# Causal mask as a matrix product, and q and k turned by DMA, in a fused decoder layer

## The chip, the cores and the metric

One core of one Trainium2 chip runs the whole layer. The metric is device time in microseconds (us) of one launch. A core has a tensor engine (PE), a vector engine (DVE), a scalar engine (ACT), GpSimd (POOL) and a sync engine (SP) that only issues transfers. Each engine works through its own instructions in the order in which they stand; ACT, SP and POOL also issue transfers (DMAs), each from its own queue. What an engine waits for at the head of its queue holds up everything behind it.

## What is computed

The layer has 1024 positions of width 1024. What matters here is its attention part: 8 heads of 64, in float32, with normalised q and k, a forget term added to the scores, a causal mask and a softmax.

```python
h = rms_norm(x, attn_norm_g)
q, k, v, f_logit, cb, cc, cu, ga, gb = jnp.split(h @ w_in, offs, axis=-1)
q = rms_norm(q.reshape(b, s, 8, 64), q_norm_g)
k = rms_norm(k.reshape(b, s, 8, 64), k_norm_g)
c = jnp.cumsum(log_sigmoid(f_logit + b_f), axis=1)
logits = einsum('bhqd,bhkd->bhqk', q, k) * 64 ** -0.5
logits = logits + (c[..., :, None] - c[..., None, :])
logits = where(key_pos <= q_pos, logits, -1e30)
y_att = einsum('bhqk,bhkd->bhqd', softmax(logits), v)
y_conv = cb * causal_short_conv(cc * cu, conv_w)
x = x + (sigmoid(ga) * (y_att @ w_out_att) + sigmoid(gb) * (y_conv @ w_out_conv)) @ w_o
```

A mixture of 16 experts and a gated embedding follow; the change does not touch them.

## The kernel before

Every float32 product is made of fp16 products: a value is split into a high and a low fp16 part (`split`, L113: ACT rounds, DVE takes the rest). The stage in question fills the first 480 us of the run.

**Blocks.** `project` (L224) makes q, k and v for one pair of heads and 128 tokens: 24 products of 384 columns into one PSUM bank named acc (two such banks). ACT squares q and k (L235), DVE sums (L237) and scales (L110), POOL takes the power -0.5 (L111), DVE writes the normalised `qn` (L240), then ACT and DVE write V (L243, L244). V at L244 is the last reader, and frees the bank. There are 32 blocks, 8 for each of 4 pairs; the first 8 run ahead of the loop over units.

**Turning q and k.** For every second block, `finish` (L249) has PE turn the two `qn` tiles, which are float32, with four transposes of 128x128 into a bank named tr. Six ACT and six DVE instructions then write Qh, Ql and K with a head's dimensions along partitions, the gains folded in (L259 to L265).

**Units.** `attend_s` (L298) makes the scores of one head and 256 queries; there are 32 units. SP loads a row of forget terms from memory to all partitions: `base` (three buffers) and again `own` (one buffer) for the half of the queries whose last 128 keys end earlier. POOL adds the causal mask to `own` (L306), DVE to `base` (L307). PE makes two products for each piece of up to 512 keys (L319, L320) into one of three banks named s; DVE adds base or own and takes the row maximum in the same instruction (L321); ACT takes the exponential (L330). Each half then has its own reciprocal (L331, L332), a split into `hl` (L335, L336) and a DMA transpose on SP into `pTr` (L338). `attend_v` (L341) multiplies pTr by V two units later.

**Filler.** `filler` (L444) interleaves products of 512 columns for the convolution and gates, L122 to L124, in runs of 24 that use the same two acc banks. Their weights (`fraw`, two buffers, L404) and the weights of the next pair (`wraw`, three buffers, L207) are loaded on SP too.

**Order.** In this stage the program is handed to a scheduler that interleaves the generators' work and fixes one order for each engine before the run. The loop that feeds it stands at L507 to L527:

```python
for n in range(len(units)):
    fills.append(scores(n + 2))
    proj = block_in(n + LEAD)
    fills.append(block_out(n + LEAD - 1))
    fills.append(itertools.islice(extra, 8 * fill_halves(n)))
    weave(values(n), units[n][1] + 1, itertools.chain(*fills), total)
```

So a block is projected eight turns of the loop ahead (LEAD = 8), and scores are made two units ahead.

Of the kernel before, what the change touches and what calls it, by code (L numbers as in the profile page):

```python
# [19 lines left out]
S = 1024  # L20
D = 1024
# [22 lines left out]
OWN = 1  # L44
# [5 lines left out]
QS = 16.0  # L50
KS = 4.0
# [5 lines left out]
NEG = -1e30  # L57


QNB = 3  # L60
# [3 lines left out]
def trunk_layer(ctx: ExitStack, tc: tile.TileContext, x, wq0, wq, wc, wgb, wga, wA, wB, wo, wr,  # L64
# [25 lines left out]
    gq = const.tile([128, 1], F32, name="gq")  # L90
    nc.vector.tensor_scalar(gq, vt[:, 0:1], DH ** -0.5 * QS, None, op0=ALU.mult)
    gk = const.tile([128, 1], F32, name="gk")
    nc.vector.tensor_scalar(gk, vt[:, 1:2], KS, None, op0=ALU.mult)
# [83 lines left out]
    mask = ap_.tile([128, 128], F32, name="mask")  # L177
    nc.gpsimd.memset(mask, 0.0)
    nc.gpsimd.affine_select(mask, mask, pattern=[[-1, 128]], compare_op=ALU.is_ge, fill=NEG,
                            base=0, channel_multiplier=1)  # L180

    def tokens_load(t):
        xt = ap_.tile([128, D], F32, name="P", bufs=5)
        nc.sync.dma_start(xt, x[t * 128:(t + 1) * 128, :])
        return xt
# [12 lines left out]
    def wq_raw(p, k):  # L198
        if p == 0 and k > 2:
            raw = (ap_.tile([128, S], F32, name="hl", bufs=3) if k < 6 else  # L200
                   ap_.tile([128, 2 * S], F32, name="pTr", bufs=3))[:, :392]
# [22 lines left out]
    def project(p, t, w, ws, V, fz):  # L224
# [13 lines left out]
        rsqrt(ss[:, 4:8], ss[:, 0:4], DH, [128, 4], EPS * PS * PS)  # L238
# [8 lines left out]
        st8["qn", p * NT + t] = qn  # L247

    def finish(s, qns, Qh, Ql, K):  # L249
        tok = slice(s * 256, (s + 1) * 256)  # L250
        tr = tr_bank()
        t4 = tr.rearrange("p (n t) -> p n t", n=2)
        for i, qn in enumerate(qns):
            for n in range(2):
                nc.tensor.transpose(t4[:, n, i * 128:(i + 1) * 128],
                                    qn[:, 2 * n:2 * n + 2].rearrange("p h d -> p (h d)"), identF)
        for hd in range(2):
            a, b = [slice(64 * i, 64 * i + 64) for i in (hd, 1 - hd)]
            nc.scalar.activation(Qh[a, hd], t4[a, 0], AF.Copy, scale=gq[a])  # L259
            nc.vector.scalar_tensor_tensor(Ql[a, hd], t4[a, 0], gq[a], Qh[a, hd], op0=ALU.mult, op1=ALU.subtract)  # L260
            nc.scalar.activation(K[a, hd, tok], t4[a, 1], AF.Copy, scale=gk[a])
            nc.vector.scalar_tensor_tensor(K[b, hd, tok], t4[a, 1], gk[a], K[a, hd, tok],
                                           op0=ALU.mult, op1=ALU.subtract)
            nc.scalar.activation(Qh[b, hd], Qh[a, hd], AF.Copy)
            nc.vector.tensor_copy(Ql[b, hd], Ql[a, hd])  # L265

    def forget(hf, fz):
# [18 lines left out]
        rows = [ap_.tile([128, S], F32, name="P", bufs=5) for _ in range(2)]  # L286
# [11 lines left out]
    def attend_s(p, s, hd, Qh, Ql, K):  # L298
# [3 lines left out]
        last = chunks(s, 0)[-1][0]  # L302
        w = 256 * s + 128 - last
        own = ap_.tile([128, 384], F32, name="own", bufs=OWN)
# [3 lines left out]
        pT_ = ap_.tile([128, 8, 2, 256], FP16, name="pTr", bufs=3)  # L308
        for i in range(2):
            qt = 2 * s + i  # L310
            nk = (qt + 1) * 128
            pt = ap_.tile([128, S], F32, name="P", bufs=5)
            st = ap_.tile([128, 8], F32, name="st", bufs=4)
            q = slice(i * 128, (i + 1) * 128)
            nch = 0
            for c0, cw in chunks(s, i):
                valid = min(cw, nk - c0)
                sb = s_bank()
                nc.tensor.matmul(sb[:, :cw], lhsT=Qh[:, hd, q], rhs=K[:, hd, c0:c0 + cw], start=True, stop=False)  # L319
                nc.tensor.matmul(sb[:, :cw], lhsT=Ql[:, hd, q], rhs=K[:, hd, c0:c0 + cw], start=False, stop=True)  # L320
                nc.vector.tensor_tensor_reduce(  # L321
                    out=pt[:, c0:c0 + valid], in0=sb[:, :valid], in1=own[:, :valid] if i == 0 and c0 == last else base[:, c0:c0 + valid], scale=1.0,
                    scalar=-3e38, op0=ALU.add, op1=ALU.max, accum_out=st[:, nch:nch + 1])
                nch += 1
                yield cw
            if nch == 2:
                nc.vector.tensor_scalar(st[:, 2:3], st[:, 0:1], st[:, 1:2], -1.0 / (QS * KS), op0=ALU.max, op1=ALU.mult)  # L327
            else:
                nc.vector.tensor_scalar(st[:, 2:3], st[:, 0:1], -1.0 / (QS * KS), None, op0=ALU.mult)
            nc.scalar.activation(pt[:, :nk], pt[:, :nk], AF.Exp, bias=st[:, 2:3], scale=1.0 / (QS * KS), accum_out=st[:, 3:4])  # L330
            nc.vector.tensor_scalar(st[:, 4:5], st[:, 3:4], 1.0 / GS, None, op0=ALU.mult)  # L331
            nc.vector.reciprocal(st[:, 5:6], st[:, 4:5])  # L332
            hl = ap_.tile([128, 8, 2, 128], FP16, name="hl", bufs=3)
            p3 = pt[:, :nk].rearrange("p (k m) -> p k m", m=128)
            nc.scalar.activation(hl[:, :qt + 1, 0], p3, AF.Copy, scale=st[:, 5:6])  # L335
            nc.vector.scalar_tensor_tensor(hl[:, :qt + 1, 1], p3, st[:, 5:6], hl[:, :qt + 1, 0], op0=ALU.mult,  # L336
                                           op1=ALU.subtract)
            nc.sync.dma_start_transpose(pT_[:, :qt + 1, :, q], hl[:, :qt + 1].rearrange("p k a m -> p (k a m)"))  # L338
        st8["P", p * 8 + 2 * s + hd] = pT_

    def attend_v(p, s, hd, P, V):  # L341
# [9 lines left out]
        yl = ap_.tile([128, 256], F32, name="yl", bufs=1)  # L351
# [10 lines left out]
    def block_in(m):  # L362
        p, t = blocks[m]
        if t == 0:
            W8[p] = load_wq(p, raw0 if p == 0 else None)
            st8["K", p] = ap_.tile([128, 2, S], FP16, name="K", bufs=2)
            st8["V", p] = ap_.tile([128, 2, 8, 128], FP16, name="V", bufs=2)
        if t % 2 == 0:
            s = t // 2
            st8["Q", p, s] = (ap_.tile([128, 2, 256], FP16, name="Qh", bufs=4),  # L370
                              ap_.tile([128, 2, 256], FP16, name="Ql", bufs=4))
            if p == 0 and s % 2 == 0:
                st8["f", s // 2] = ap_.tile([128, 4, 8], F32, name="fz", bufs=2)
        yield from project(p, t, *W8[p], st8["V", p], st8.get(("f", t // 4)))

    def block_out(m):
        p, t = blocks[m]
        if t % 2:
            finish(t // 2, [st8.pop(("qn", i)) for i in (m - 1, m)], *st8["Q", p, t // 2], st8["K", p])
# [3 lines left out]
        if t % 2:  # L383
            yield 430

    def scores(n):
        p, s, hd = units[n]
        yield from attend_s(p, s, hd, *st8["Q", p, s], st8["K", p])
# [82 lines left out]
    for i in range(WARM):  # L471
        nc.tensor.matmul(warm[:, :128], lhsT=identB, rhs=identB, start=True, stop=True)
    for t in range(2):
# [35 lines left out]
    for n in range(len(units)):  # L509
# [843 lines left out]
def layouts(i):  # L1353
# [49 lines left out]
    o["gains"] = np.stack([a["attn_norm_g"][0], a["ffn_norm_g"][0]])  # L1403
# [24 lines left out]
```

## Time and profile before

| | |
|---|---|
| median of 3 runs | 1128.04 us (1127.67 to 1128.4) |
| time of the profiled execution | 1129.68 us |
| its span in the trace | 1128.0 us |
| PE busy | 1051.3 us (93%) |
| DVE busy | 709.2 us (63%) |
| ACT busy | 563.5 us (50%) |
| POOL busy | 189.4 us (17%) |

The span is what the trace covers; 1.7 us lie around it. A matmul's busy time is modelled and overlaps with the next one's, so the cost of one matmul in a row of them is read from the distance of two starts. The granted clock of PE is given as a share: 1.00 is 2.4 GHz and 0.50 is 1.2 GHz. In the timeline the brackets hold the time that the engine stood idle before the instruction, and what ended it. The line numbers are those of the kernel before.

### The profile page before, as it was taken

The page shows a single profiled execution, that of the slowest core. Times are in us where ns is not written, and L with a number is a line of the kernel's source. Part 1 is how long each engine was busy: PE and PEld are TensorE (multiplying, and loading weights), DVE is VectorE, ACT ScalarE, POOL GpSimd, SP SyncE. Part 2 cuts the span into 40 slices and gives each one's busy share as a digit, 9 for nine tenths or more (in the row PEclk, how much of TensorE's full clock was granted, in tenths as well). Part 3 has the DMA queues.
Part 4 walks back from the last instruction along what each step waited for, and adds up shares of the span by engine and source line. Part 5 has one row for each costly group of instructions (what it writes and reads, how often), then busy time and mean ns, then how long its engine had stood idle before and what let it go on. Part 6 is the DMA issues. An engine that isn't in the chain of part 4 may idle for free. (4 is left out here: it accounts for less than half of the span.)

```text
span 1128.0 us, 18292 instructions
## 1 busy us (share of the span) xinstructions
PE 1051.3 (93%) x6776; PEld 607.1 (54%) x6776; DVE 709.2 (63%) x1603; ACT 563.5 (50%) x1033; POOL 189.4 (17%) x247
## 2 busy tenths in 40 slices
PE   7878998998999999999998999987989999998798
PEld 5544454554455544444443355546766777764354
DVE  7777765677766764032307745874978888855633
ACT  7665455565554653222215433445766777753232
POOL 3311011111211000000003422242201111005300
PEclk9979898999999999999999999988989999999999
DMA  8055456565665583152348650149999899727511
GB/s 310 24 129 143 105 124 157 126 129 138 152 129 117 138 179 93 53 176 87 112 154 259 207 211 38 57 135 371 388 383 302 306 334 325 236 78 235 180 53 56
DMA packets 135135, 195.46 MB, mean 173 GB/s; under 512 B 83010, under 2 KB 94794, under 8 KB 134914
## 3 DMA queue, kind: packets, MB, share of 16 engines
q1 hardware_dynamic: 118290, 141.40, 42.9%
q0 software_dynamic: 7632, 27.07, 7.3%
q10 hardware_dynamic: 9120, 25.78, 5.9%
q8 instruction: 54, 0.88, 0.3%
q14 instruction: 39, 0.32, 0.1%
HBM read 142.75 MB, written 32.59 MB: 155 GB/s over the span
## 5 line engine op out<-in xcount | busy, mean ns | idle before, releaser
L122 PE MATMUL acc<-hTh,fwh 128*128 128x512 f16 x336 | 127.3, 379 | 0.1
L124 PE MATMUL acc<-hTh,fwl 128*128 128x512 f16 x336 | 127.3, 379 | 0.0
L123 PE MATMUL acc<-hTl,fwh 128*128 128x512 f16 x336 | 127.3, 379 | 0.0
L961 DVE SCALAR_TENSOR_TENSOR wl<-wraw,wh 128x1024 f16<-128x1024 f32 x64 | 77.5, 1219 | 23.9 <-ACT wh L956 23.2
L230 PE MATMUL acc<-wqh,hTh 128*128 128x384 f16 (+1 forms) x248 | 83.0, 335 | 7.0 <-DVE V L244 4.7
L116 DVE SCALAR_TENSOR_TENSOR wl<-wraw,wh 128x1024 f16<-128x1024 f32 x47 | 57.4, 1232 | 51.0 <-ACT wh L115 49.5
L231 PE MATMUL acc<-wqh,hTl 128*128 128x384 f16 (+1 forms) x248 | 83.0, 335 | 0.8 <-DVE hTl L116 0.8
L232 PE MATMUL acc<-wql,hTh 128*128 128x384 f16 (+1 forms) x248 | 83.0, 334 | 0.2 <-DVE wql L116 0.2
L956 ACT ACTIVATE wh<-wraw 128x1024 f16<-128x1024 f32 x64 | 66.9, 1052 | 19.5 <-PE acc L1041 10.6
L330 ACT ACTIVATE P<-P,st 128x128 f32<-128x128 f32 (+3 forms) x64 | 49.2, 769 | 50.5 <-DVE st L327 38.2
L115 ACT ACTIVATE wh<-wraw 128x1024 f16<-128x1024 f32 x47 | 49.1, 1054 | 50.2 <-PE acc L123 26.4
L335 ACT ACTIVATE hl<-P,st 128x128 f16<-128x128 f32 (+3 forms) x64 | 48.8, 770 | 38.4 <-issue 15.8
L336 DVE SCALAR_TENSOR_TENSOR hl<-P,st,hl 128x128 f16<-128x128 f32 (+3 forms) x64 | 52.0, 818 | 12.6 <-ACT hl L335 12.2
L1324 PE MATMUL acc<-wh,xl 128*128 128x512 f16 (+1 forms) x136 | 50.4, 371 | 5.7 <-DVE xl L116 5.7
L1041 PEld LDWEIGHTS <-wh 128*128 128x128 f16 x512 | 51.5, 101 | 4.2 <-issue 0.8
L124 PEld LDWEIGHTS <-fwl 128*128 128x128 f16 x336 | 32.9, 98 | 38.3
L1040 PEld LDWEIGHTS <-wh 128*128 128x128 f16 x512 | 52.1, 102 | 1.9 <-issue 0.3
L111 POOL TENSOR_TENSOR ss<-ss,mh 128x4 f32<-128x4 f32 x32 | 37.6, 1176 | 91.5 <-DVE ss L110 87.3
L122 PEld LDWEIGHTS <-fwh 128*128 128x128 f16 x336 | 32.9, 98 | 34.8
L123 PEld LDWEIGHTS <-fwh 128*128 128x128 f16 x336 | 32.9, 98 | 34.5 <-issue 0.3
L1325 PE MATMUL acc<-wl,xh 128*128 128x512 f16 (+1 forms) x136 | 50.4, 370 | 0.0
L1323 PE MATMUL acc<-wh,xh 128*128 128x512 f16 (+1 forms) x136 | 50.4, 370 | 0.0
(319 smaller groups left out, 2621.8 us busy)
## 6 DMA issues: line engine op xcount, KB each, us to landing
wraw<-in_we_dram SPq DMA_DIRECT2D x96, 512.0 KB
Yd<-yt ACTq DMA_DIRECT2D x14, 512.0 KB
fraw<-in_wc_dram SPq DMA_DIRECT2D x12, 512.0 KB
wraw<-in_wq_dram SPq DMA_DIRECT2D x24, 192.0 KB
P<-in_x_dram SPq DMA_DIRECT2D x8, 512.0 KB
fraw<-in_wga_dram SPq DMA_DIRECT2D x8, 512.0 KB
base<-brow SPq DMA_DIRECT2D x8, 512.0 KB
sga<-fg POOLq DMA_DIRECT2D x8, 512.0 KB, 5.9
```

Of the source, the lines that this page charges most:

```text
L116: nc.vector.scalar_tensor_tensor(lo, src, scale, hi, op0=ALU.mult, op1=ALU.subtract)
L122: nc.tensor.matmul(acc, lhsT=whi, rhs=xhi, start=k == 0, stop=False)
L123: nc.tensor.matmul(acc, lhsT=whi, rhs=xlo, start=False, stop=False)
L124: nc.tensor.matmul(acc, lhsT=wlo, rhs=xhi, start=False, stop=k == nk - 1)
L230: nc.tensor.matmul(acc[:, :w], lhsT=hTh[:, k, tok], rhs=wh[:, :w], start=k == 0, stop=False)
L231: nc.tensor.matmul(acc[:, :w], lhsT=hTl[:, k, tok], rhs=wh[:, :w], start=False, stop=False)
L232: nc.tensor.matmul(acc[:, :w], lhsT=hTh[:, k, tok], rhs=wl[:, :w], start=False, stop=k == 7)
L336: nc.vector.scalar_tensor_tensor(hl[:, :qt + 1, 1], p3, st[:, 5:6], hl[:, :qt + 1, 0], op0=ALU.mult, op1=ALU.subtract)
L956: nc.scalar.activation(wh, raw, AF.Copy, scale=HS)
L961: V_.scalar_tensor_tensor(wl, raw, HS, wh, op0=ALU.mult, op1=ALU.subtract)
L1040: nc.tensor.matmul(a[:, :n], lhsT=wh[:, k], rhs=xT[:, k, 0, :n], start=k == 0, stop=False)
L1041: nc.tensor.matmul(a[:, :n], lhsT=wh[:, k], rhs=xT[:, k, 1, :n], start=False, stop=False)
```

## The change

Four edits go together.

1. **q and k in rows.** The transposes and splits of `finish` are gone. `project` now scales and splits q and k while tokens lie along partitions: POOL multiplies `qn` by a gain tile, ACT and DVE write `rows`, fp16 of 128 x 768 (six groups of 128 columns; k's gain is folded into q's), and one DMA transpose on SP for each block writes them into `KQ`. The scaling at L110 moves from DVE to POOL for these blocks.
2. **Mask as a product.** A matrix of -60000 above the diagonal is multiplied by 60000 times the identity and added to the scores in PSUM by one product of 128 columns for each half unit. `own` is gone, with its load, and so are both mask additions.
3. **Queues.** The loads of `base`, of the filler's weights and of the next pairs' weights are issued on POOL instead of SP.
4. **Smaller ones.** The reciprocals of a unit's two halves are one instruction of two columns; `P` has 4 buffers for 5, `hl` 2 for 3, `qn` 2 for 3; scale factors QS and KS change places.

```diff
-    def finish(s, qns, Qh, Ql, K):
...
-                nc.tensor.transpose(t4[:, n, i * 128:(i + 1) * 128],
-                                    qn[:, 2 * n:2 * n + 2].rearrange("p h d -> p (h d)"), identF)
...
-            nc.scalar.activation(Qh[a, hd], t4[a, 0], AF.Copy, scale=gq[a])
-            nc.vector.scalar_tensor_tensor(Ql[a, hd], t4[a, 0], gq[a], Qh[a, hd], op0=ALU.mult, op1=ALU.subtract)
...
-        rsqrt(ss[:, 4:8], ss[:, 0:4], DH, [128, 4], EPS * PS * PS)
+        rsqrt(ss[:, 4:8], ss[:, 0:4], DH, [128, 4], EPS * PS * PS, nc.gpsimd)
...
+        nc.gpsimd.tensor_tensor(qn, qn, gqk, op=ALU.mult)
+        rows = ap_.tile([128, 2, 3, 2, DH], FP16, name="rows", bufs=2)
+        nc.scalar.activation(rows[:, :, 0, 0], qn[:, 2:4], AF.Copy)
+        nc.vector.tensor_tensor(rows[:, :, 0, 1], qn[:, 2:4], rows[:, :, 0, 0], op=ALU.subtract)
+        q2 = qn[:, 0:2, None, :].to_broadcast([128, 2, 2, DH])
+        nc.scalar.activation(rows[:, :, 1], q2, AF.Copy)
+        nc.vector.tensor_tensor(rows[:, :, 2], q2, rows[:, :, 1], op=ALU.subtract)
+        nc.sync.dma_start_transpose(KQ[:, :, tok], rows.rearrange("p h j a d -> p (h j a d)"))
...
-        nc.sync.dma_start(base[:, :n], brow[s][2 * p + hd:2 * p + hd + 1, :].to_broadcast([128, n]))
...
-        nc.sync.dma_start(own[:, :w], brow[s][2 * p + hd:2 * p + hd + 1, last:last + w].to_broadcast([128, w]))
-        nc.gpsimd.tensor_tensor(own[:, w - 128:w], own[:, w - 128:w], mask, op=ALU.add)
-        nc.vector.tensor_tensor(base[:, n - 128:n], base[:, n - 128:n], mask, op=ALU.add)
+        nc.gpsimd.dma_start(base[:, :n], brow[s][2 * p + hd:2 * p + hd + 1, :].to_broadcast([128, n]))
...
+                end = c0 + cw == nk
+                nc.tensor.matmul(sb[:, :cw], lhsT=KQ[:, 3 * hd + 1, q], rhs=KQ[:, 3 * hd, c0:c0 + cw], start=True, stop=False)
+                nc.tensor.matmul(sb[:, :cw], lhsT=KQ[:, 3 * hd + 2, q], rhs=KQ[:, 3 * hd, c0:c0 + cw], start=False, stop=not end)
+                if end:
+                    nc.tensor.matmul(sb[:, cw - 128:cw], lhsT=identM, rhs=mask, start=False, stop=True)
...
-            nc.sync.dma_start(raw[:, :384], wq[p - 1, :, k, :])
+            nc.gpsimd.dma_start(raw[:, :384], wq[p - 1, :, k, :])
...
-            nc.sync.dma_start(FR[i], wc[j, "CUB".index(kind)] if kind in "CUB" else (wga if kind == "g" else wgb)[j])
+            nc.gpsimd.dma_start(FR[i], wc[j, "CUB".index(kind)] if kind in "CUB" else (wga if kind == "g" else wgb)[j])
```

How the scheduled order moves, at three places. PE first, at a place late in pair 0: the last scores of a unit (L319, L320), the turn of q and k, and the first products of the next block (L230). Before:

```order
L320 MATMUL s<-K,Ql 128x384
L319 LDWEIGHTS Qh
L319 MATMUL s<-K,Qh 128x512
L320 LDWEIGHTS Ql
L320 MATMUL s<-K,Ql 128x512
L255 MATMUL tr<-identF,qn 128x128 x2
L230 LDWEIGHTS hTh
L230 MATMUL acc<-wqh,hTh 128x384
```

After the change, where scores of the same kind end and the values of an earlier unit follow (L302, L303 are the score products, L305 the mask):

```order
L302 LDWEIGHTS KQ
L302 MATMUL s<-KQ 128x512
L303 LDWEIGHTS KQ
L303 MATMUL s<-KQ 128x512
L305 LDWEIGHTS identM
L305 MATMUL s<-mask,identM 128x128
L335 LDWEIGHTS V
L335 MATMUL o<-pTr,V 128x256
```

The transposes of `qn` are gone from PE everywhere; 64 products of the mask stand behind the score products.

SP, where eight weight tiles of a later pair are loaded (L301 and L305 load base and own, L207 and L404 weights). Before:

```order
L301 DMA base<-brow_73 128x768
L305 DMA own<-brow_72 128x384
L207 DMA wraw<-in_wq_dram 128x384 x3
L338 DMA_TRANSPOSE pTr<-hl 128x4x128
L207 DMA wraw<-in_wq_dram 128x384 x5
L338 DMA_TRANSPOSE pTr<-hl 128x6x128
L301 DMA base<-brow_73 128x768
L404 DMA fraw<-in_wc_dram 128x1024
L338 DMA_TRANSPOSE pTr<-hl 128x8x128
```

After, SP at about the same place (L324 is the old L338, L252 the new transpose):

```order
L324 DMA_TRANSPOSE pTr<-hl 128x2x128
L324 DMA_TRANSPOSE pTr<-hl 128x4x128
L252 DMA_TRANSPOSE KQ<-rows 128x6x128
L324 DMA_TRANSPOSE pTr<-hl 128x6x128
L324 DMA_TRANSPOSE pTr<-hl 128x8x128
```

Only transposes are left on SP in this stage, but for the loads at its start.

POOL at the same load of weights. Before, one mask addition and one power for each turn of the loop, and a store of a gate (L423):

```order
L306 TENSOR_TENSOR own<-own,mask 128x128
L111 TENSOR_TENSOR ss<-ss,mh 128x4
L423 DMA sga<-fg 128x1024
L111 TENSOR_TENSOR ss<-ss,mh 128x4
L306 TENSOR_TENSOR own<-own,mask 128x128
L111 TENSOR_TENSOR ss<-ss,mh 128x4
```

After (L288 loads base, L205 and L384 weights; L105 and L106 are the scaling and the power, L245 the gain):

```order
L288 DMA base<-brow_73 128x768
L205 DMA wraw<-in_wq_dram 128x384 x3
L105 TENSOR_SCALAR ss<-ss 128x4
L106 TENSOR_TENSOR ss<-ss,mh 128x4
L205 DMA wraw<-in_wq_dram 128x384 x2
L245 TENSOR_TENSOR qn<-qn,gqk 128x256
L205 DMA wraw<-in_wq_dram 128x384 x3
L403 DMA sga<-fg 128x1024
L384 DMA fraw<-in_wc_dram 128x1024
L288 DMA base<-brow_73 128x768
L105 TENSOR_SCALAR ss<-ss 128x4
```

The scaling and power of a block, which the block's acc bank waits for, now stand behind loads that may have to wait for a buffer.

## Rows read from the trace of the kernel before

**Rows 1.** Stretches: us; busy PE, PEld, DVE, ACT, POOL; clock, DMA share, GB/s.
```profile
0.00:51.40 51.40, 43.47 (x300) 29.70 (x301) 39.16 (x92) 34.39 (x87) 15.57 (x27) 1.00 0.50 181
...
72.00:120.00 48.00, 40.70 (x217) 21.40 (x216) 38.41 (x121) 27.72 (x62) 5.93 (x8) 0.93 0.62 149
...
200.00:450.00 250.00, 244.74 (x1375) 132.03 (x1373) 168.85 (x488) 137.58 (x279) 29.38 (x40) 1.00 0.59 135
```

**Rows 2.** Waits of PE from 51 to 450 us: total, times, longest.
```profile
PE tr L255 <- DVE qn L240: 10.8, 5, 4.4
...
PE acc L230 <- DVE V L244: 4.7, 9, 1.2
```

**Rows 3.** Timeline, PE, the two longest waits of the loop over units.
```profile
114.85 0.69 PE L255 MATMUL tr<-identF,qn 128*128 128x128 f32 x2 [4.05 <-DVE qn L240]
116.09 0.48 PE L230 MATMUL acc<-wqh,hTh 128*128 128x384 f16 x1 [0.55 <-DVE cu L429]
...
190.21 0.69 PE L255 MATMUL tr<-identF,qn 128*128 128x128 f32 x2 [4.41 <-DVE qn L240]
```

**Rows 4.** Stretches in which PE had the lower clock, columns as in rows 1.
```profile
55.00:68.70 13.70, 8.15 (x30) 4.77 (x30) 8.09 (x34) 6.06 (x18) 4.51 (x6) 0.50 0.39 87
113.10:119.90 6.80, 4.49 (x15) 2.15 (x16) 6.26 (x17) 1.91 (x4) 0.00 (x0) 0.50 0.67 129
188.20:195.00 6.80, 4.64 (x15) 2.35 (x16) 5.38 (x21) 4.74 (x12) 1.48 (x2) 0.50 0.41 107
```

**Rows 5.** Timeline, SP and DVE, ahead of the wait at 190 us.
```profile
178.65 0.57 SPq L301 DMA_DIRECT2D base<-brow  x1
...
185.13 0.29 DVE L307 TENSOR_TENSOR base<-base,mask 128x128 f32<-128x128 f32 x1 [5.67 <-DMA base<-brow]
```

**Rows 6.** Timeline, PE: starts of transposes and of products of 128 columns.
```profile
46.59 0.60 PE L255 MATMUL tr<-identF,qn 128*128 128x128 f32 x4
47.02 0.33 PE L230 MATMUL acc<-wqh,hTh 128*128 128x392 f16 x1
...
51.44 0.22 PE L319 MATMUL s<-K,Qh 128*128 128x128 f16 x1
51.50 0.22 PE L320 MATMUL s<-K,Ql 128*128 128x128 f16 x1
```

**Rows 7.** Timeline, PE and POOL, at the first scores.
```profile
54.38 0.27 PE L319 MATMUL s<-K,Qh 128*128 128x256 f16 x1 [2.66 <-ACT s L145]
...
59.31 0.37 PE L319 MATMUL s<-K,Qh 128*128 128x256 f16 x1 [3.98 <-DVE st L321]
...
64.08 0.58 PE L319 MATMUL s<-K,Qh 128*128 128x512 f16 x1 [1.44 <-DVE st L321]
...
63.24 0.45 POOL L306 TENSOR_TENSOR own<-own,mask 128x128 f32<-128x128 f32 x1 [3.81 <-DMA own<-brow]
```

**Rows 8.** Groups to 480 us: busy us, mean ns, idle before.
```profile
L260 DVE SCALAR_TENSOR_TENSOR Ql<-tr,gq,Qh 64x256 f16<-64x256 f32 x32 | 15.4, 480 | 1.2 <-ACT Qh L259 0.3
...
L240 DVE TENSOR_TENSOR qn<-acc,ss 128x256 f32<-128x256 f32 x31 | 13.1, 422 | 10.7 <-POOL ss L111 7.0 <-PE acc L123 1.2 <-PE s L320 1.2
...
L111 POOL TENSOR_TENSOR ss<-ss,mh 128x4 f32<-128x4 f32 x32 | 37.6, 1176 | 91.5 <-DVE ss L110 87.3 <-DVE ft L271 4.0
L306 POOL TENSOR_TENSOR own<-own,mask 128x128 f32<-128x128 f32 x32 | 16.2, 507 | 194.1 <-DMA own<-brow 133.7 <-DVE hl L336 17.9 <-DVE st L332 15.5
L423 POOL DMA_DIRECT2D sga<-fg x8 | 4.9, 608 | 38.7 <-ACT fg L421 38.7
```

**Rows 9.** One line: the DMA transposes on SP, ns min/median/max.
```profile
L338 SPq DMA_TRANSPOSE pTr<-hl x64: 1174/1325/2948, 65.0 to 432.0; - x64
```

**Rows 10.** Timeline, POOL and SP: the start, and the loads of a pair's weights.
```profile
6.89 0.56 POOL L111 TENSOR_TENSOR rn_ss<-rn_ss,mh 128x1 f32<-128x1 f32 x1 [4.34 <-DVE rn_ss L110]
...
10.29 0.85 SPq L404 DMA_DIRECT2D fraw<-in_wc_dram  x2
...
171.91 5.42 SPq L207 DMA_DIRECT2D wraw<-in_wq_dram  x5
```

More of the change, by code (lines that the diff above doesn't have):

```diff
@@ L49 @@
 XS = 16.0
-QS = 16.0
-KS = 4.0
+QS = 4.0
+KS = 16.0
 GS = 4096.0
@@ L56 @@
 POB = 4
-NEG = -1e30
-QNB = 3
+MASK = 60000.0
+QNB = 2
 @with_exitstack
@@ L199, in wq_raw @@
         if p == 0 and k > 2:
-            raw = (ap_.tile([128, S], F32, name="hl", bufs=3) if k < 6 else
+            raw = (ap_.tile([128, S], F32, name="hl", bufs=2) if k < 5 else
                    ap_.tile([128, 2 * S], F32, name="pTr", bufs=3))[:, :392]
@@ L285, in forget @@
                                      0.0 if hf == 0 else cs[:, c0 - 1:c0], op0=ALU.mult, op1=ALU.add)
-        rows = [ap_.tile([128, S], F32, name="P", bufs=5) for _ in range(2)]
+        rows = [ap_.tile([128, S], F32, name="P", bufs=4) for _ in range(2)]
         c0s = ap_.tile([8, 4], F32, name="c0s", bufs=1)
@@ L321, in attend_s @@
+                if end:
+                    nc.tensor.matmul(sb[:, cw - 128:cw], lhsT=identM, rhs=mask, start=False, stop=True)
                 nc.vector.tensor_tensor_reduce(
-                    out=pt[:, c0:c0 + valid], in0=sb[:, :valid], in1=own[:, :valid] if i == 0 and c0 == last else base[:, c0:c0 + valid], scale=1.0,
-                    scalar=-3e38, op0=ALU.add, op1=ALU.max, accum_out=st[:, nch:nch + 1])
-                nch += 1
+                    out=pt[:, c0:c0 + valid], in0=sb[:, :valid], in1=base[:, c0:c0 + valid], scale=1.0,
+                    scalar=-3e38, op0=ALU.add, op1=ALU.max, accum_out=st[:, 1 if c0 else 0, i:i + 1])
@@ L332, in attend_s @@
[L332 to L338, printed above, removed]
+            if c0:
+                nc.vector.tensor_scalar(st[:, 2, i:i + 1], st[:, 0, i:i + 1], st[:, 1, i:i + 1], -1.0 / (QS * KS), op0=ALU.max, op1=ALU.mult)
+            else:
+                nc.vector.tensor_scalar(st[:, 2, i:i + 1], st[:, 0, i:i + 1], -1.0 / (QS * KS), None, op0=ALU.mult)
@@ new lines, in attend_s @@
+            nc.scalar.activation(pt[:, :nk], pt[:, :nk], AF.Exp, bias=st[:, 2, i:i + 1], scale=1.0 / (QS * KS), accum_out=st[:, 3, i:i + 1])
+        nc.vector.tensor_scalar(st[:, 4], st[:, 3], 1.0 / GS, None, op0=ALU.mult)
+        nc.vector.reciprocal(st[:, 4], st[:, 4])
+        for i in range(2):
+            qt = 2 * s + i
+            r = st[:, 4, i:i + 1]
+            hl = ap_.tile([128, 8, 2, 128], FP16, name="hl", bufs=2)
+            p3 = pts[i][:, :(qt + 1) * 128].rearrange("p (k m) -> p k m", m=128)
+            nc.scalar.activation(hl[:, :qt + 1, 0], p3, AF.Copy, scale=r)
+            nc.vector.scalar_tensor_tensor(hl[:, :qt + 1, 1], p3, r, hl[:, :qt + 1, 0], op0=ALU.mult, op1=ALU.subtract)
+            nc.sync.dma_start_transpose(pT_[:, :qt + 1, :, i * 128:(i + 1) * 128],
+                                        hl[:, :qt + 1].rearrange("p k a m -> p (k a m)"))
@@ L365, in block_in @@
             W8[p] = load_wq(p, raw0 if p == 0 else None)
-            st8["K", p] = ap_.tile([128, 2, S], FP16, name="K", bufs=2)
+            st8["KQ", p] = ap_.tile([128, 6, S], FP16, name="KQ", bufs=2)
             st8["V", p] = ap_.tile([128, 2, 8, 128], FP16, name="V", bufs=2)
[L368 to L374, printed above, removed]
+        if p == 0 and t % 4 == 0:
+            st8["f", t // 4] = ap_.tile([128, 4, 8], F32, name="fz", bufs=2)
+        yield from project(p, t, *W8[p], st8["V", p], st8.get(("f", t // 4)), st8["KQ", p])
     def block_out(m):
         p, t = blocks[m]
-        if t % 2:
-            finish(t // 2, [st8.pop(("qn", i)) for i in (m - 1, m)], *st8["Q", p, t // 2], st8["K", p])
         if p == 0 and t % 4 == 3:
@@ L472, in trunk_layer @@
         nc.tensor.matmul(warm[:, :128], lhsT=identB, rhs=identB, start=True, stop=True)
+    for i in range(4):
+        j = 2 + (i > 1)
+        nc.gpsimd.dma_start(gqk[:, i], gains[j:j + 1, 0:DH].to_broadcast([128, DH]))
+    gk2 = gqk[:, 2:4]
+    nc.gpsimd.tensor_tensor(gqk[:, 0:2], gqk[:, 0:2], gk2, op=ALU.mult)
+    nc.gpsimd.tensor_scalar(gqk[:, 0:2], gqk[:, 0:2], DH ** -0.5 * QS, 0.0, op0=ALU.mult, op1=ALU.add)
+    nc.gpsimd.memset(gk2, KS)
     for t in range(2):
```

66 lines of the change are left out of this document (21 added, 45 removed).

## The prediction, made before the result was known

> **What bounds the kernel now.** I read the table of stretches first. From 200 to 450 us PE is busy for 244.74 of 250 us at the full clock [rows 1], while DVE stands at two thirds: the stage is bound by PE, and whatever PE no longer does or waits for shortens it. The first 120 us are less full: PE is busy for 43.47 of 51.40 us, and later 40.70 of 48 us at a mean clock of 0.93 [rows 1]. Next come the waits of PE. The largest is the turn of q and k: five times, 10.8 us in all, PE stood at a transpose until DVE had written qn; nine shorter waits, 4.7 us, were for the acc bank, which V at L244 frees [rows 2]. The timeline shows the two longest, 4.05 and 4.41 us, and another wait of 0.55 us right behind the first [rows 3]. Around each lies a stretch of 6.8 us at half clock, in which PE was busy for 4.49 and 4.64 us [rows 4]. Then I asked why qn was late. Ahead of the wait at 190 us DVE stood for 5.67 us at L307, waiting for the load of base, which SP had issued only at 178.65 us [rows 5], because it stood behind weight loads that took SP 5.42 us [rows 10]. So SP's order delays base, base delays DVE, DVE delays qn, and qn holds PE.
>
> After 450 us nothing changes. PE goes on without a break from this stage into the next, so I let a gain or loss pass to the end one to one.
>
> **The change part by part.** The sum goes against the profiled execution, 1129.68 us; it lies 1.64 us above the median, and I subtract the same sum from the median.
>
> Transposes on PE. Four take from 46.59 to 47.02 us, 0.108 us each [rows 6]; 64 of them are 6.9 us. Two products of 128 columns start 0.06 us apart [rows 6], so 64 products with the mask add 3.8 us. Net gain 3.1 us, all of it in PE's own time.
>
> Waits at the transposes. With the instruction the 10.8 us of waiting [rows 2] go, and half of the 9.1 us that PE worked at half clock [rows 4], 4.6 us: at most 15.4 us. Below, nothing may come of it, if PE stops a little later for the same late DVE. I take 11 us, nearer the top, since what made DVE late goes too: SP keeps only transposes in this stage, L307 is gone, and so are three DVE instructions for each half of `finish`, the first of them 480 ns [rows 8], 32 times. What DVE gets instead, two subtractions for each block, are no larger than its 422 ns for 256 columns [rows 8]. ACT loses six instructions for two blocks and gets four. Both engines become lighter; neither is the bound, so I count nothing for that itself.
>
> First scores. PE waited 2.66, 3.98 and 1.44 us there, 8.1 in all, while POOL waited 3.81 us for a load of own [rows 7]; own has one buffer, so its loads follow each other. The stretch at half clock held 8.15 us of work [rows 4], which cost 4.1 us. At most 12.2 us can go; nothing need, since base still has to be written to memory and read back. I take 5 us, less than half: the two waits for DVE, 5.4 us, hang on own or base, and the first, for ACT, stays.
>
> The rsqrt chain. A block's scaling moves from DVE to POOL and stands there behind transfers. POOL's power takes 1176 ns for four columns, an addition of 128 columns 507 ns [rows 8]; the added scaling of four columns should lie under that, some 0.4 us. A transfer issued on POOL takes 608 ns [rows 8]. If the nine acc waits [rows 2] each grow by both, 1.0 us, that is 9 us; if the lighter DVE is sooner by as much, nothing or a small gain. I take a loss of 2 us, nearer the lower end, as most blocks have some time in hand. The gain multiplication stands behind the power and not on the way to the acc bank.
>
> DMA transposes. The old ones take SP 1325 ns in the median [rows 9]; 32 more are 42 us of issue, in a queue that loses 109 loads. A block is projected eight turns ahead, so its KQ has several turns to land. I count zero; if that cover were gone, each late one would cost up to its own 1.3 us, 42 us in all. DMA's share is 0.59 [rows 1], so there is room. Loads of base have three buffers and stand on POOL two or more units ahead: zero too.
>
> The start. POOL stood idle for 4.34 us before its first power [rows 10]. Six transfers at 608 ns and the making of the scaled identity, by the 507 ns row, are 4.2 us and just fit. But two tiles of the filler's weights, 1.05 MB, are now asked for before 10.29 us [rows 10], beside the tokens. At the 181 GB/s of this stretch [rows 1] they hold back the tokens by 5.8 us at most, and by nothing if the tokens were in time. I take 2 us.
>
> Smaller edits (fewer buffers, reciprocals in one) I count as zero: the buffers still cover two units.
>
> Sum: -3.1 - 11 - 5 + 2 + 2 = -15.1 us. Against 1129.68 that is 1114.6 us; from the median 1128.04 it is **1113 us**.
>
> **The rivals.** *POOL's queue becomes the gate (slower).* Its place is the change of pairs: eight weight loads stand on POOL around the scaling and power of a block. On SP five of them took 5.42 us [rows 10], 1.1 us each, because they wait for a buffer. On POOL eight would hold the queue for 8.8 us, and half of it, 4.4 us, can fall before a power. Then the acc bank is late, PE waits as it did at 114.85 us [rows 3], and the clock drops, which cost some 2.3 us each time [rows 4]. Three pairs make 3 x 6.7 = 20 us, and nine blocks with 0.6 us more, 5.4 us in place of my 2, another 3.4: 1113 + 23.4 = 1136 us. It decides from the point at which a power stands behind waiting loads for longer than the run of filler products in the other acc bank. For it speaks the order of POOL, against it that the scheduler split the eight loads into groups around the power.
>
> The Trainium skill, page "SBUF — State Buffer", section "SBUF: two separate sides", would make this rival likelier: it says that GpSimd writes the descriptors of the transfers it issues, and is locked out of doing so while DVE runs an instruction that takes both ports, such as a float32 copy. The section after it gives 620 ns alone and about 3100 ns beside such a copy; over 77 moved loads that would be an estimated 191 us more on POOL. The trace does not show it: eight issues on POOL took 608 ns in the mean [rows 8] with DVE busy for two thirds of the time [rows 1]. By the row the sum stands; by the rule the rival's 1136 us or more would be the forecast. I leave the rival at 0.14.
>
> *The wait moves on.* Right behind the wait of 4.05 us PE waited another 0.55 us for the acc bank [rows 3], so DVE was late for more than qn. If DVE stays late, PE stops at the bank instead of the transpose, and of the 11 us nothing is gained; with 2 us instead of 5 at the first scores it is -3.1 - 2 + 2 + 2 = -1.1, 1127 us, and with half of the 11 us kept 1121 us. Against it: base no longer waits in SP's queue.
>
> *All waits go.* With the full 15.4 and 12.2 us and no loss, 1128.04 - 30.7 = 1097 us. It would need the path of the forget rows through memory to be hidden at the first scores.
>
> **How the numbers follow.** About 0.2% (2.3 us) is what a measurement of this kernel can tell from no change. My forecast, 1104 to 1121 us, gets 0.5; all waits gone, 1097 to 1104, 0.12; the wait that moves on, 1121 to 1128, 0.22, of which 0.14 lies below 1125.7 us; POOL's gate, 0.14, slower; small losses without a name, 1130 to 1133, 0.02. That gives faster 0.76, same 0.08, slower 0.16. The range 1098 to 1130 us leaves out POOL's gate and little else.
>
> **What would show it.** Right: no wait of PE over 1.5 us between 75 and 450 us, no stretch at half clock after the first scores, DVE's waits for base mostly gone, SP's waits all at transposes. The scores' first stage should hold less than 8.1 us of waiting. Wrong: PE waiting at L228 for the acc bank with POOL's L106 as the cause, long idle times of POOL ahead of weight loads, scores waiting for KQ, or PE's first products later by more than 4 us.

## The result and the profile after

| | before | after |
|---|---|---|
| median | 1127.86 us (1121.22 to 1128.4, 4 runs) | 1111.8 us (1109.74 to 1114.68, 4 runs) |
| profiled execution, its span | 1129.68, 1128.0 us | 1110.83, 1109.1 us |

The ratio is 0.9886, with a 95% interval from 0.9854 to 0.9918: the change is faster by about 1.1%. The time forecast was 1113 us. The sum was right, but several of its terms were not, and the reason given for the largest one was wrong. So the interest lies in how the parts behave alone.

The stretches of the kernel after, columns as in rows 1, and below them the three stretches in which PE had the lower clock:

```profile
0.00:51.40 51.40, 37.26 (x249) 25.35 (x250) 32.77 (x71) 29.42 (x78) 27.23 (x50) 0.90 0.57 185
...
72.00:120.00 48.00, 43.88 (x239) 23.12 (x238) 31.21 (x97) 23.03 (x58) 16.05 (x26) 0.93 0.67 151
...
200.00:450.00 250.00, 250.00 (x1416) 134.22 (x1415) 150.09 (x386) 125.13 (x256) 52.35 (x82) 1.00 0.59 133
...
13.40:23.60 10.20, 5.43 (x19) 3.05 (x20) 6.31 (x13) 6.56 (x17) 2.23 (x5) 0.50 0.84 323
61.20:71.40 10.20, 5.97 (x27) 3.96 (x27) 6.19 (x26) 6.25 (x20) 6.31 (x9) 0.50 0.41 96
81.70:88.50 6.80, 5.90 (x15) 1.98 (x15) 4.77 (x15) 2.21 (x8) 2.83 (x5) 0.50 0.91 201
```

Beside [rows 1], PE is now busy for all of 200 to 450 us, and DVE falls from 168.85 to 150.09 us there. But the first 51.4 us got worse: PE is busy for 37.26 us in place of 43.47, and from 13.4 to 23.6 us it has the lower clock (0.50, 1.2 GHz), which the kernel before did not have there. Just before, PE had stood from the end of its warm-up products at 8.4 us to 14.76 us.

The waits of PE in the kernel after, from 9 to 450 us (total, times, longest):

```profile
PE tr L156 <- DVE P L149: 6.4, 1, 6.4
PE s L302 <- DVE st L306: 4.2, 1, 4.2
...
PE s L302 <- ACT s L140: 2.7, 1, 2.7
PE acc L228 <- ACT wqh L110: 1.5, 1, 1.5
```

The first stands at the very start, the next two at the first scores. Behind 75 us nothing over 1.5 us is left of what [rows 2] showed.

To see where the time went I read the same four marks from the timeline of PE in every kernel: the first product of `project`, the first scores, the first product of the filler, and the first product of the stage behind (s from bmh, 478.63 us before). From there to the end it is 649.4 us before and 648.3 after, so nearly all of the difference lies ahead of that mark.

| kernel | first product | first scores | first filler | end of stage | filler to end |
|---|---|---|---|---|---|
| before | 10.18 | 51.44 | 79.81 | 478.63 | 398.8 |
| after | 19.87 | 58.11 | 83.78 | 460.78 | 377.0 |

The start lost 6.7 us up to the first scores, the way from there to the filler gained 2.7, and the long part behind gained 21.8.

### The profile page after: what moved, and what is told of

Same layout as the page of the kernel before. It is cut to its first block, busy times and chain, and to the rows that moved or that the text cites. A ratio compares the mean times of both kernels' runs of the same rounds, so it can differ in the third digit from the quotient of the medians.

```text
span 1109.1 us, 18207 instructions
## 1 busy us (share of the span) xinstructions
PE 1042.5 (94%) x6776; PEld 602.0 (54%) x6776; DVE 674.2 (61%) x1441; ACT 538.9 (49%) x1001; POOL 253.1 (23%) x364
## 3 DMA queue, kind: packets, MB, share of 16 engines
q0 software_dynamic: 15136, 53.42, 15.4%
## 5 line engine op out<-in xcount | busy, mean ns | idle before, releaser
L947 DVE SCALAR_TENSOR_TENSOR wl<-wraw,wh 128x1024 f16<-128x1024 f32 x64 | 77.4, 1218 | 21.8 <-ACT wh L942 21.8
L230 PE MATMUL acc<-wql,hTh 128*128 128x384 f16 (+1 forms) x248 | 81.8, 330 | 1.1 <-DVE wql L111 1.1
L110 ACT ACTIVATE wh<-wraw 128x1024 f16<-128x1024 f32 x47 | 49.1, 1054 | 55.9 <-PE acc L118 27.5
L306 DVE CUSTOM_DVE_ANT_0 P<-s,base 128x512 f32<-128x512 f32 (+2 forms) x96 | 51.2, 552 | 24.4 <-PE s L305 19.4
L322 ACT ACTIVATE hl<-P,st 128x128 f16<-128x128 f32 (+3 forms) x64 | 46.5, 767 | 13.7 <-ACT P L314 8.4
L991 POOL DMA_INDIRECT xg<-h2d,toki x16 | 18.1, 1131 | 145.0 <-PE tr L1006 135.7
```

The lines of the kernel that those rows point to most:

```text
L230: nc.tensor.matmul(acc[:, :w], lhsT=hTh[:, k, tok], rhs=wl[:, :w], start=False, stop=k == 7)
L947: V_.scalar_tensor_tensor(wl, raw, HS, wh, op0=ALU.mult, op1=ALU.subtract)
```

## The experiments

Each is set against the kernel before, timed beside it, whose median lay between 1127.07 and 1128.16 us. The intervals are about 0.2 to 0.5% to each side, most of them wider than the 0.2% that the prediction took. The marks and waits come from one profiled execution of each kernel. Three theories opened the study. Q is the one of the prediction: the order of SP makes base late, base delays DVE, DVE delays qn. T: PE waits only because the transposes stand in its order. M: the mask edit, that is own's single buffer and the mask additions, is what delays DVE.

### The edits apart

**Only the queues**, on the kernel before (three loads moved):

```diff
-            nc.sync.dma_start(raw[:, :384], wq[p - 1, :, k, :])
+            nc.gpsimd.dma_start(raw[:, :384], wq[p - 1, :, k, :])
-        nc.sync.dma_start(base[:, :n], brow[s]...)
+        nc.gpsimd.dma_start(base[:, :n], brow[s]...)
-            nc.sync.dma_start(FR[i], ...)
+            nc.gpsimd.dma_start(FR[i], ...)
```

> The kernel before (1127.9 us) with the three kinds of load (base, the filler's weights, the next pairs' weights) on POOL's queue and nothing else. Theory Q (SP's order makes base late, base delays DVE, DVE delays qn): most waits at the transposes go, less some 5 us at the start: 1114 to 1120 us. Theory T (PE waits because the transposes stand in its order; where the loads are issued does not matter): no gain and the loss at the start, 1128 to 1133 us. Theory M (the single buffer of own and the two mask additions delay DVE): as T, 1128 to 1133 us.

**Only the mask as a product**, on the kernel before, loads on SP: L302 to L307 go, and behind L320 stands

```diff
+                if end:
+                    nc.tensor.matmul(sb[:, cw - 128:cw], lhsT=identM, rhs=mask, start=False, stop=True)
```

> The kernel before with the mask as a product, without own and the mask additions, loads still on SP. Theory Q: the waits for base stay; 3.8 us of products more, a few us less at the first scores: 1124 to 1130 us. Theory T: 1126 to 1132 us. Theory M: nearly all of the gain, 1110 to 1116 us.

**Both of these**, with the turn of q and k still on PE:

> The kernel before with the mask as a product and the loads on POOL; q and k still turned by PE. Theory Q: close to the change but for 6.9 us of transposes, 1113 to 1119 us. Theory T: the transposes and their waits are still there, 1126 to 1134 us. Theory M: 1113 to 1119 us.

**The change with its three loads back on SP** (the turn by DMA, the mask as a product):

> The change (1111.8 us) with the three kinds of load back on SP. Theory Q: SP's order holds base back again, now behind 32 more transposes; only PE's own work and the clock are gained: 1120 to 1130 us. Theory T: the whole gain without the loss at the start, 1103 to 1108 us. Theory M: as T, 1103 to 1108 us.

| kernel | median us | ratio to before, 95% | first scores | first filler | filler to end |
|---|---|---|---|---|---|
| queues alone | 1144.46 | 1.0142 (1.0114 to 1.0169) | 54.02 | 87.05 | 400.6 |
| mask alone | 1114.01 | 0.9871 (0.9845 to 0.9898) | 51.68 | 80.39 | 383.2 |
| mask and queues | 1118.32 | 0.9924 (0.9892 to 0.9957) | 54.55 | 83.91 | 380.3 |
| turn and mask, loads on SP | 1110.91 | 0.9858 (0.983 to 0.9886) | 57.80 | 84.24 | 377.2 |

Theory Q's remedy failed at once. The queue edit alone made the kernel slower by 17 us, where Q had put it at 1114 to 1120 us and T and M at 1128 to 1133 us, and DVE waited as long as ever for base, whose load was now issued on POOL. Waits from 75 to 450 us in this run, DVE first, then PE, then POOL:

```profile
DVE base L307 <- DMA base<-brow: 31.7, 23, 3.6
...
PE tr L255 <- DVE qn L240: 10.9, 7, 4.9
...
POOL own L306 <- DMA own<-brow: 75.4, 23, 8.3
...
POOL fraw L404 <- DVE fwl L116: 39.1, 9, 12.2
POOL base L301 <- DVE st L321: 24.0, 10, 5.6
```

In the kernel before, same stretch:

```profile
DVE base L307 <- DMA base<-brow: 31.2, 20, 5.7
```

The loads now stand on POOL behind its own waits for own and for free buffers. So the run shows that moving the load does not bring base sooner; what PE would do with base in time and the mask addition still on DVE, no run shows. Little of the loss lies in the long stage: of the 14.8 us by which the profiled span grew, 7.2 had come by the first filler, under 2 came in the stage, and 5.8 behind it, in code that no edit touches and that took from 646.3 to 655.2 us in the kernels of this study.

T fell too: in the kernel with only the mask edit all transposes of qn are still on PE, yet of PE's 10.8 us of waits there [rows 2] one of 1.0 us is left:

```profile
PE tr L257 <- DVE qn L242: 1.0, 1, 1.0
```

The stage from the first filler to its end is 15.6 us shorter with the mask edit alone, though PE does 64 products more. The two marks, before, then with the mask alone:

```profile
79.81 0.38 PE L122 MATMUL acc<-hTh,fwh 128*128 128x512 f16 x1
...
478.63 0.39 PE L122 MATMUL s<-bmh,wh 128*128 128x512 f16 x1 [1.63 <-ACT wh L115]
```

```profile
80.39 0.38 PE L122 MATMUL acc<-hTh,fwh 128*128 128x512 f16 x1
...
463.59 0.39 PE L122 MATMUL s<-bmh,wh 128*128 128x512 f16 x1 [1.63 <-ACT wh L115]
```

The turn by DMA, with the smaller edits, takes off another 6.0 us (383.2 to 377.2), close to the 6.9 us of transposes on PE, and the queue edit 0.2 us (377.2 to 377.0). So M was right that it is the mask edit. M, like T, missed the last run of the four all the same: 1110.91 us in place of 1103 to 1108, because the gain tile's loads still stood on POOL there (see "The start"). What of the mask edit does it was tried next.

### Inside the mask edit

**Two buffers for own** on the kernel before (yl shares the buffers of sq to make room):

```diff
-OWN = 1
+OWN = 2
```

> The kernel before with two buffers for own instead of one (the buffer of yl is shared with sq to make room), nothing else. Theory O: SP stands at the load of own (34.0 us, 17 times in the kernel before) until the unit before has read the one buffer, and base loads and transposes behind it are late; with two buffers these waits go, PE's waits at the transposes of qn fall under 4 us, and the time is 1113 to 1120 us. Theory L: what makes qn late is that DVE's mask addition L307 waits in DVE's order for a base that is late anyway; then DVE's 31 us of waits for base stay, PE's waits stay at 8 to 12 us, and the time is 1124 to 1131 us.

**The mask addition into base on POOL** in place of DVE, nothing else:

```diff
-        nc.vector.tensor_tensor(base[:, n - 128:n], base[:, n - 128:n], mask, op=ALU.add)
+        nc.gpsimd.tensor_tensor(base[:, n - 128:n], base[:, n - 128:n], mask, op=ALU.add)
```

> The kernel before with the mask addition into base (L307) on POOL instead of DVE; own, its one buffer, its load and its own mask addition stay. Theory L: DVE no longer waits for base ahead of qn, PE's waits at the transposes fall under 4 us, and the time is 1112 to 1120 us. Theory O: base and own come as late as before, DVE stands at L321 instead of L307, PE's waits stay over 7 us and the time is 1123 to 1132 us.

Two buffers gave 1130.53 us, ratio 1.0037 (1.0016 to 1.0057): O fell. Moving one addition of 0.29 us [rows 5] for each unit gave 1115.79 us, ratio 0.9901 (0.987 to 0.9931): all but some 2 us of what the mask edit gains. The marks agree: from the first filler to the end of the stage it is 398.8 us with two buffers, as before, and 383.2 us with the addition on POOL, as with the mask edit. The first fence is the kernel with two buffers (waits of SP, DVE and PE from 75 to 450 us), the second the one with the addition on POOL (POOL and PE):

```profile
SPq L305 <- DVE st L321: 15.8, 11, 3.5
...
DVE base L307 <- DMA base<-brow: 41.0, 27, 4.6
...
PE tr L255 <- DVE qn L240: 10.1, 7, 3.3
```

```profile
POOL base L307 <- DMA base<-brow: 67.5, 21, 7.5
...
PE tr L255 <- DVE qn L240: 5.1, 3, 1.9
```

With two buffers SP's wait at the load of own fell (28.2 us in 15 waits before, same stretch), and DVE's wait for base grew. With the addition on POOL it is POOL that stands for base. DVE's waits for POOL's power at qn even rise, from 7.0 to 20.3 us, and yet PE's waits at the transposes halve (to 5.1 us, not under 4 as L had said). That looked like L: an instruction that waits for a late load, early in the order of DVE. So the last test put such a wait back without the work.

**The mask edit, and a copy of one column of base on DVE where L307 stood:**

```diff
+        jk = ap_.tile([128, 1], F32, name="jk", bufs=2)
+        nc.vector.tensor_copy(jk, base[:, n - 1:n])
```

> The second run of the first call (mask as a product on the kernel before, loads on SP) with one more DVE instruction for each unit: a copy of one column of base into a tile that nothing reads, where L307 stood. Theory L says that not the mask addition's own time but its wait for base in DVE's order makes qn late: 32 copies of about 0.1 us bring back DVE's waits for base (20 us or more), PE's waits at the transposes (over 7 us) and 1121 to 1129 us. If it was the mask addition's work, or own's traffic on SP, the time stays at 1112 to 1117 us.

It took 1115.04 us, ratio 0.9904 (0.9869 to 0.9939): the miss of theory L. The waits of DVE came back as foreseen, those of PE did not (waits of DVE, then PE, 75 to 450 us):

```profile
DVE jk L305 <- DMA base<-brow: 33.3, 23, 4.5
...
PE tr L257 <- DVE qn L242: 2.7, 3, 1.8
...
PE tr L257 <- DVE st L332: 1.3, 1, 1.3
```

So 33 us of waiting for base on DVE are not enough to hold PE. From ACT's square of a block (L235) to the end of its qn (L240), read from the timeline over 28 or 29 blocks, it takes 4.21 us in the mean in the kernel before, 4.64 with the queue edit alone, 4.06 with the addition on POOL, 3.99 with the one-column copy and 3.57 with the mask edit. These differ by about 1 us; PE only meets the few blocks in which several delays come together. In the kernel before that was 5.67 us for base at once [rows 5] at the wait of 190 us, but 1.36 us for base and a row of other work at that of 115 us. Which of the delays has to go is thus not one thing: either the addition off DVE (own still there) or own and the addition's work off (a wait for base still there) was enough. DVE is busy for 168.85 us of 200 to 450 us before [rows 1], for 165.9 to 168.3 us in the other slow kernels of this study, and for 159.0 to 163.0 us in the three fast ones that keep the turn on PE and the loads on SP. So DVE's load may decide. But in a shorter kernel the same 250 us hold another part of the stage, each edit also makes the scheduler set a new order, and no run holds the order and changes the load alone. Whether it is the load or the order stays open.

### The start

**The six early loads of POOL back on SP**, in the kernel after (the gain tile's four, and the first two of the filler's weights):

```diff
-        nc.gpsimd.dma_start(gqk[:, i], gains[j:j + 1, 0:DH].to_broadcast([128, DH]))
+        nc.sync.dma_start(gqk[:, i], gains[j:j + 1, 0:DH].to_broadcast([128, DH]))
-            nc.gpsimd.dma_start(FR[i], ...)
+            (nc.sync if i < 2 else nc.gpsimd).dma_start(FR[i], ...)
```

> The kernel after with the four loads of the gain tile and the first two loads of the filler's weights back on SP, behind the first token loads; all else as in the change. Theory S1: these six transfers on POOL at the start are what moved the first token's scaling on DVE behind the weight splits and made the weight tiles land late; the first transposes come at 8.8 to 10 us instead of 14.76, the first scores at 52 to 54 instead of 58.11, and the time is 1104 to 1108 us. Theory S2: the start is set by the path of the forget rows, and its gain is taken back at the first scores; the first filler stays at 83 to 85 us and the time is 1109 to 1113 us.

**The same, and the eighth token's load on POOL**:

> As the run before, and the load of the eighth token tile issued on POOL instead of SP, where it stood behind five transposes of KQ. If that load is what makes base late at the first scores, PE's wait of 4.23 us for DVE there falls under 2 us and the time is 2 to 4 us under the run before, 1101 to 1105 us. If base is late for its own way through memory, the time is within 1.5 us of the run before.

**Only the filler's two loads back on SP**, the gain tile on POOL:

> The kernel after with only the first two loads of the filler's weights back on SP; the gain tile's four loads stay on POOL. Theory G (the gain tile's loads are enough to put the first scaling behind weight splits on DVE): the first transposes come at 11 to 13 us, time 1107 to 1111 us. Theory F (the filler's weights, 1.05 MB beside the tokens, are the whole loss): first transposes at 8.8 to 10 us, 1104 to 1107 us.

| kernel | median us | ratio to before, 95% | first transposes | first scores | first filler |
|---|---|---|---|---|---|
| after | 1111.8 | 0.9886 (0.9854 to 0.9918) | 14.76 | 58.11 | 83.78 |
| fill on SP | 1108.32 | 0.9849 (0.9796 to 0.9903) | 12.32 | 56.27 | 81.97 |
| fill and gain on SP | 1105.57 | 0.9815 (0.9762 to 0.9868) | 8.87 | 51.85 | 77.89 |
| the same, eighth token on POOL | 1109.15 | 0.9842 (0.9811 to 0.9873) | 8.81 | 52.05 | 77.84 |

The marks say it more sharply than the medians, whose intervals overlap: both sets of loads take part, and with both on SP the start is where it was before, as S1 had it. What the gain tile's four loads cost alone can be read from two other runs that differ in nothing else: base and all weights are loaded on SP, and the gain tile on POOL ("turn and mask, loads on SP" above) or on SP too (the first run of the next section). The first transposes of the two:

```profile
12.16 1.61 PE L156 MATMUL tr<-identF,P 128*128 128x128 f32 x8 [4.19 <-DVE P L149]
...
8.79 1.09 PE L156 MATMUL tr<-identF,P 128*128 128x128 f32 x8 [1.47 <-DVE P L149]
```

The first filler comes at 84.24 and 77.44 us, and the medians are 1110.91 and 1102.25 us, with intervals of the ratio that do not touch (0.983 to 0.9886 and 0.9759 to 0.9828).

The timeline of the kernel after shows how the start is lost. The first token's power is ready on POOL at 7.4 us, but on DVE its scaling L149 stands behind four weight splits, and their tiles land late:

```profile
4.94 1.09 POOL L384 DMA_DIRECT2D fraw<-in_wc_dram  x2
...
6.84 0.58 POOL L106 TENSOR_TENSOR rn_ss<-rn_ss,mh 128x1 f32<-128x1 f32 x1 [0.31 <-DVE rn_ss L105]
...
9.32 0.53 ACT L110 ACTIVATE wqh<-wraw 128x392 f16<-128x392 f32 x1 [2.94 <-DMA wraw<-in_wq_dram]
...
12.38 0.53 ACT L110 ACTIVATE wqh<-hl 128x392 f16<-128x392 f32 x1 [1.07 <-DMA hl<-in_wq_dram]
...
13.43 1.28 DVE L149 SCALAR_TENSOR_TENSOR P<-P,rn_ss,base 128x1024 f32<-128x1024 f32 x1
14.76 1.97 PE L156 MATMUL tr<-identF,P 128*128 128x128 f32 x8 [6.38 <-DVE P L149]
```

With the six loads on SP behind the first tokens the order on DVE has L149 ahead of the splits again (why the scheduler turns this order round, no run shows):

```profile
8.87 1.09 PE L156 MATMUL tr<-identF,P 128*128 128x128 f32 x8 [0.45 <-DVE P L149]
10.22 0.34 PE L228 MATMUL acc<-wqh,hTh 128*128 128x392 f16 x1 [0.25 <-ACT hTh L110]
```

The eighth token's load was a miss: PE's wait at the first scores was 4.0 us with it and 4.2 us without, and the median is 3.6 us above that of the run without, inside the spread of its runs (1100.95 to 1111.97 us). What makes base late there was not found; its way through memory is the guess left.

### What the queues are worth

**The whole change with all of these loads on SP**, the gain tile's too:

> The change with base, both kinds of weights and the gain tile all loaded on SP, so that nothing of the queue edit is left. If the queue edit is worth nothing once the start is in order: 1103 to 1108 us, with PE busy for all of 200 to 450 us and the first transposes at 8.8 to 10 us. If POOL's queue is what keeps the stage full: waits of PE come back between 75 and 450 us and the time is 1110 to 1118 us.

**Only the queues, on the kernel before, with the filler's first two loads on SP:**

> The first run of the first call (only the queue edit, on the kernel before) with the first two loads of the filler's weights back on SP. If its loss of 17 us was that start: 1126 to 1134 us, first scores at 51 to 52 us. If it lies in the stage behind, where POOL's loads wait for buffers ahead of powers and of the masks of own: 1138 to 1146 us.

The first took 1102.25 us, ratio 0.9793 (0.9759 to 0.9828), the fastest of all and just under the 1103 to 1108 us expected if the queue edit is worth nothing: the change without its queue edit. Its stage from the filler to the end is 373.5 us. Of the 3.5 us to the kernel after, an estimated 2.4 us are clock: there PE worked for 4.80 us at half the clock from 83.7 to 88.5 us, of which half would be saved, while here the clock is 1.00 from 72 to 120 us. PE hardly waits (the stretch with columns as in rows 1, and the longest waits of PE from 40 to 450 us):

```profile
200.00:450.00 250.00, 249.11 (x1396) 132.37 (x1393) 143.09 (x368) 120.64 (x246) 34.17 (x48) 1.00 0.57 129
...
PE s L302 <- DVE st L306: 3.5, 2, 2.7
PE s L302 <- ACT s L140: 2.9, 2, 2.7
PE acc L228 <- ACT wqh L110: 1.8, 2, 1.3
```

Against the kernel with only the six loads moved (0.9815) the intervals overlap; a gain from the queue edit is not to be seen in either. The second took 1140.28 us, ratio 1.0136 (1.0094 to 1.0178): on the kernel before, the loss of the queue edit does not come from those two loads. Its first product came at 10.06 us, its first scores at 55.46 and its first filler at 85.89, and PE's waits at the transposes and for acc's bank were 9.0 and 7.2 us. Some 4 us are lost by the first scores, 2 more by the filler and 3.2 in the stage; the rest, 1.4 us of the profiled span, lies behind it and was not followed. So the time fell into the second range, but the stage, where that range had put the loss, holds less than a third of it.

## Why the prediction was right in sum

**Right.** PE's own work: two products with the mask start 0.06 us apart in the kernel after, as taken from [rows 6], and the turn by DMA took 6.0 us off the stage against the 6.9 us counted for the transposes. DMA transposes at zero: none of the 96 pairs of score products waited for a transpose of KQ, which took SP 1.22 us in the median and landed 2.8 us after its issue. A block's scaling on POOL held nothing up: DVE waited 11.5 us for POOL's power at qn, 15 times, the longest 1.4 us, but PE's waits behind V for acc's bank came to 0.6 us. Of the signs of being right, no wait of PE over 1.5 us, the waits for base (DVE once, 1.2 us, from 75 to 450 us) and the waits at the first scores (6.9 us) came as named; one did not: PE had the lower clock again from 81.7 to 88.5 us, behind the first scores.

**Mis-sized: the waits at the transposes.** The step "I take 11 us" had a top of 15.4 us. Together with PE's own -3.1 and the chain's +2 that made -12.1 for the stage; it gained 21.8. The sums of the stretches from 80 us to the end of the stage show what the bound left out, before, with the mask alone, and after (stretch, then PE's busy time):

```profile
sum 398.00, PE 380.46 PEld 203.88 DVE 254.16 ACT 207.35 POOL 48.38; mean PE 47.56 PEld 25.49 DVE 31.77 ACT 25.92 POOL 6.05
```

```profile
sum 383.00, PE 378.07 PEld 205.95 DVE 248.24 ACT 207.35 POOL 33.25; mean PE 47.26 PEld 25.74 DVE 31.03 ACT 25.92 POOL 4.16
```

```profile
sum 380.00, PE 375.91 PEld 201.65 DVE 230.62 ACT 190.36 POOL 94.17; mean PE 46.99 PEld 25.21 DVE 28.83 ACT 23.80 POOL 11.77
```

PE stood for 17.5 us before (398.00 less 380.46), 4.9 with the mask alone and 4.1 after. The bound counted the waits named at the transposes and two stretches of lower clock, but not the waits for acc's bank, 4.7 us [rows 2], which hang on the same DVE: of these 0.6 us is left. The top of 15.4 and these 4.7 make 20.1 us; the mask alone took off 19.4 (15.6 and the 3.8 us of its products).

**Wrong: the cause.** Of "SP's order delays base, base delays DVE, DVE delays qn" the first link gave no remedy: with base issued on POOL DVE waited as long for it (31.7 us after 31.2), PE as long at the transposes (10.9 us after 10.8), and the kernel was slower. That SP's order made base late in the kernel before [rows 5] is not refuted by this. As the whole cause it failed at the second link: with 33 us of waits for base, but without the mask addition's work and without own, DVE did not hold PE. The place, qn at the transposes, and the engine, DVE, were right. The edit that helped was the mask, which the prediction had named only in passing ("L307 is gone").

**Wrong: the first scores.** The term was -5 us. With the mask alone PE's waits there were 6.2 and 2.8 us, against 5.4 and 2.9 before, so nothing went, as the lower bound had it: own was not what they hung on. In the kernel after they are 4.2 and 2.7 us, and the way to the filler is 2.7 us shorter.

**Mis-sized: the start.** The term was +2 us with a top of 5.8; it was +6.7 by the first scores. The bound counted only bytes beside the tokens. The other half was an order: with these loads on POOL the scheduler placed the first scaling behind weight splits on DVE, and after the gap PE also had the lower clock. "PE's first products later by more than 4 us" was named as a sign of wrong, and they came 9.7 us later. It was noted as a sign and then priced at 2.

So the number came out right partly by luck, since errors of opposite sign met: the stage gave 9.7 us more than forecast, the start took 4.7 more and the first scores gave 2.3 less.

**The rivals.** POOL as the gate did not happen in the changed kernel, though its sign did: POOL stood 54.0 us ahead of filler weights, 13 times, up to 12.8 us, and PE waited for acc's bank no longer than 1.5 us at a time. On the kernel before, the same loads cost 17 us (1144.46 us), but the waits by which a gate would show did not grow: PE waited 10.9 us at the transposes and 3.9 us for V at acc's bank there (75 to 450 us), 10.8 and 4.7 us without the edit. The wait did not move on to the bank either, where 0.6 us is left. The issues themselves stayed short. POOL's groups to 480 us in the kernel after (busy us, mean ns, idle before):

```profile
L106 POOL TENSOR_TENSOR ss<-ss,mh 128x4 f32<-128x4 f32 x32 | 33.8, 1058 | 2.5
...
L288 POOL DMA_DIRECT2D base<-brow x32 | 18.7, 585 | 81.4 <-DVE st L311 45.2 <-DVE st L306 25.6 <-DVE st L313 6.1
L205 POOL DMA_DIRECT2D wraw<-in_wq_dram x24 | 13.4, 558 | 21.0 <-DVE wql L111 10.6 <-DVE st L313 4.4 <-DVE rows L248 1.8
L105 POOL TENSOR_SCALAR ss<-ss 128x4 f32<-128x4 f32 x32 | 7.7, 241 | 54.3 <-DVE ss L235 51.1 <-DVE c0s L277 2.7
```

An issue took 558 or 585 ns with DVE busy for 60% of 200 to 450 us, less than the 608 ns of [rows 8]. The Trainium skill, page "SBUF — State Buffer", section "SBUF: two separate sides", says that GpSimd cannot write the descriptors of a transfer issued on it while DVE runs an instruction that takes both ports, such as a float32 copy. Nothing of it shows here, in the issues or in the landings: base landed 3.3 to 4.8 us after its issue on POOL, and 2.9 to 4.8 us on SP in the version with all loads there (medians by size). But DVE runs no copy in this stage of the kernel after, so this case hardly tests the page's rule; leaving the rival small was right for this kernel. The rival in which all waits go, 1097 us, is nearly reached by the best version, at 1102.25 us.

## What to carry to other kernels

Before a wait's cause is priced, follow it with one edit at a time: here the edit thought to be the remedy, moving loads to another queue, cost 1.4% alone and added nothing in company, while taking one 0.29 us addition for each unit, and the wait in front of it, off the loaded in-order engine was worth 1%. Idle time before an instruction says what it waited for, not what that wait costs; here it cost something only where it met other delays on the way to the engine that bounds. And where a scheduler fixes the orders, a few loads placed early can reorder an unrelated engine: read the first microseconds of the new order on every engine, and price what it shows.

## What the runs showed that was not expected

A wait of 33 us on DVE, in 23 pieces, cost PE nearly nothing, while the kernel before, with nearly the same wait (31.2 us in 20 pieces), took 14 us more for the stage (398.8 and 384.5). A second buffer for own, which let SP pass, made the time no better (1.0037). And the runs of one kernel spread more than the 0.2% taken: 1100.95 to 1111.97 us in four runs of one version.
